# Merge exponents formed in the product's PSUM bank, and the masked statistics multiplied by GpSimd

## The chip, the core and the metric

The kernel runs on one core of one Trainium2 chip. The metric is the device time of one execution in microseconds; the figure of a kernel is the median of its runs. The engines are TensorE (PE, with its weight loads PEld), VectorE (DVE), ScalarE (ACT), GpSimd (POOL) and SyncE (SP), which here only issues transfers.

## The reference, cut to what matters

One decoder layer for a prompt of 2048 positions (width 1024) and a sample group of 8 x 4 positions: RMSNorm and one input projection, dilated attention with 8 heads of 64 and a spatial gating unit, an output projection, then a SwiGLU network and a final norm. In the attention each head has three branches, (window, dilation) = (128,1), (512,4), (2048,16), and merges them by their softmax denominators:

```python
def _merge_branches(outs, lses):
    w = jax.nn.softmax(jnp.stack(lses, axis=0), axis=0)
    return jnp.sum(w[..., None] * jnp.stack(outs, axis=0).astype(jnp.float32), axis=0)
```

The change touches how the weights of this merge are computed for the prompt.

## The kernel before, in words

The program has three parts in time: the projections with the sample group's attention and the gates (to about 600 us), the prompt's attention (about 600 to 975 us), and the output projection with the feed-forward network (to the end).

The prompt's attention runs head by head. Two kinds of items follow each other, one per step of a plan: a *band* item (the branches of dilation 1 and 4 together) for each of the 16 query tiles of a head, in which query rows are consecutive positions; and a *strided* item (dilation 16), four per head, each for four of the 16 residues, in which a row is a position divided by 16. For a band item TensorE forms the scores in one of two PSUM buffers ps_s (L864), VectorE adds the bias and takes the row's extremum (L870, an operation followed by a readout into the statistics st), ScalarE forms the exponential with its row sum (L875), TensorE transposes it (L891) into a PSUM bank, ScalarE and VectorE copy that out (L896, L902), and TensorE multiplies by the values (L916). For a strided item GpSimd first reorders k, qh and ql into sq (L937, three copies), TensorE forms the scores (L945), VectorE adds the bias (L950) and reduces (L952), GpSimd subtracts (L953), ScalarE takes the exponential (L956), VectorE sums (L960), TensorE transposes (L965) and multiplies (L974). A score buffer is free for the item after next when L870 (or L950) has read it.

The tile st of a head holds four statistics per row and tile: [0] and [1] for the band, by position tile, [2] and [3] for the strided branch, by residue. The class Stats brings both into one layout and computes the two merge factors of each position, in steps: **a** multiplies st[0:2], repeated eight times, by a mask sel_g into the tile sm (128 x 256, L998); **b** multiplies sm by sel_r on TensorE (L1004, four matmuls of 16 columns), which turns the band statistics into the strided layout, in one PSUM bank; **c** copies both to SBUF (s, L1008); **weights_a** forms the smaller of the two extrema and the two differences (L1014, L1015, L1016, tiles of 128 x 16); **weights_e** takes their exponentials on ScalarE (L1019); **weights_b** forms the weighted sum, its reciprocal and the two factors on VectorE (L1024 to L1028); **store** sends the factors to DRAM from ScalarE's queue (L1032). They are loaded back, spread over the partitions, by merge_load (L1042 or L1046), and merge applies them in three operations per quarter of a head (L1054, L1056, L1058), on GpSimd but for one quarter of the last head, whose result merge_store sends out on SyncE's queue (L1063).

The order is written by hand: `at(step, phase, function)` enters a call, and the calls are issued by step, then by phase (early, exp, low, scores, turn, mid, values, out, misc, store), then by entry. Each engine executes its share in that order. The statistics of a head are computed while the next head's items run; the last head's are computed in two halves, one of them during its own items. That makes nine calls.

A bank for transposes and for the product of step b comes from ps_a, which takes three banks in turn.

Of the kernel before, what the change touches and what calls it, by code (L numbers as in the profile page):

```python
# [13 lines left out]
OP = mybir.AluOpType  # L14
# [5 lines left out]
P = 128  # L20
T = 2048
NT = T // P
# [42 lines left out]
def hymba_step(ctx: ExitStack, tc: tile.TileContext, A: dict, O: dict):  # L65
    nc = tc.nc
    sync, act, dve, pool, pe = nc.sync, nc.scalar, nc.vector, nc.gpsimd, nc.tensor
# [7 lines left out]
    turn = [0, 0, 0, 0]  # L75
# [618 lines left out]
    for half in range(2):  # L694
        for ki, kind in enumerate(ORDER[half]):
            for gi, tiles in enumerate(GROUPS):
                start = ((half * 5 + ki) * 3 + gi) * 8
                for k in range(KD):
                    if start == 0:

                        for j in range(3):
                            n = 3 * k + j
# [281 lines left out]
    s12 = {}  # L984
# [3 lines left out]
    class Stats:  # L988
# [6 lines left out]
        def a(self):  # L995
            n = self.r1 // 8
            self.m = ap_.tile([P, 2 * P], F32, name="sm", tag="sm", bufs=1).rearrange("p (a n g) -> p a n g", a=2, g=8)[:, :, 0:n]
            dve.tensor_tensor(self.m, self.st["t"][:, 0:2, 0:n].unsqueeze(3).broadcast_to([P, 2, n, 8]),  # L998
                              sel_g.unsqueeze(1).unsqueeze(1).broadcast_to([P, 2, n, 8]), op=OP.mult)
# [6 lines left out]
        def c(self):  # L1006
            self.s = self.small("s12", 2)
            dve.tensor_copy(self.s.rearrange("p a t -> p (a t)"), self.p[0:self.r1, 0:2 * NT])  # L1008

        def weights_a(self):  # L1010

            m3 = self.st["t"][0:self.r1, 2, :]
            self.f = f = self.small("f", 3)
            dve.tensor_tensor(f[:, 2, :], self.s[:, 0, :], m3, op=OP.min)  # L1014
            dve.tensor_sub(f[:, 0, :], f[:, 2, :], self.s[:, 0, :])  # L1015
            dve.tensor_sub(f[:, 1, :], f[:, 2, :], m3)  # L1016
# [4 lines left out]
        def weights_b(self):  # L1021
            f, m = self.f, self.f[:, 2, :]
            dd = self.small("dd", 2)
            dve.tensor_mul(dd[:, 0, :], f[:, 0, :], self.s[:, 1, :])  # L1024
# [112 lines left out]
    def stats_of(h, steps, r0, r1):  # L1137
        d = {}
        at(*steps[0], lambda: d.update(s=Stats(h, sts[h], r0, r1)))
        for (y, ph), fn in zip(steps, "a b c weights_a weights_e weights_b store".split()):  # L1140
            at(y, ph, lambda fn=fn: getattr(d["s"], fn)())

    for h in range(H):
# [4 lines left out]
        if end:  # L1148

            x = s0 - NI  # L1150
            stats_of(h, [(x + y, ph) for y, ph in ((14, "early"), (14, "turn"), (15, "early"), (15, "misc"), (16, "early"), (16, "early"), (16, "mid"))], 0, 64)
            steps = ((2, "early"), (2, "turn"), (3, "early"), (4, "early"), (4, "early"), (5, "early"), (5, "early"))
# [6 lines left out]
        else:  # L1159
            steps = ((2, "misc"), (3, "misc"), (4, "early"), (4, "early"), (5, "early"), (5, "misc"), (6, "mid"))  # L1160
# [890 lines left out]
```

## Time and profile before

| | |
|---|---|
| median of 3 runs | 2692.8 us (2679.7 to 2697.14) |
| profiled execution, own time | 2691.25 us |
| its span, first to last instruction | 2689.5 us |
| mean granted TensorE clock | 0.967 |
| busy: PE, PEld, DVE, ACT, POOL | 2533.0, 2170.3, 1375.7, 1206.2, 1408.6 us |
| attention stage, 560 to 980 us: PE, DVE, POOL busy | 368.81, 259.14, 276.24 us |

The page is read in this way: busy time counts an instruction from its start to its end, so an instruction that stands at an engine and cannot proceed counts as busy too. Idle time ahead of a group is listed with the instruction that ended most of it. The granted clock is a share of full speed.

### The profile page before, as it was taken

The page shows a single profiled execution, that of the slowest core. Times are in us where ns is not written, and L with a number is a line of the kernel's source. Part 1 is how long each engine was busy: PE and PEld are TensorE (multiplying, and loading weights), DVE is VectorE, ACT ScalarE, POOL GpSimd, SP SyncE. Part 2 cuts the span into 40 slices and gives each one's busy share as a digit, 9 for nine tenths or more (in the row PEclk, how much of TensorE's full clock was granted, in tenths as well). Part 3 has the DMA queues.
Part 4 walks back from the last instruction along what each step waited for, and adds up shares of the span by engine and source line. Part 5 has one row for each costly group of instructions (what it writes and reads, how often), then busy time and mean ns, then how long its engine had stood idle before and what let it go on. Part 6 is the DMA issues. An engine that isn't in the chain of part 4 may idle for free. (4 is left out here: it accounts for less than half of the span.)

```text
span 2689.5 us, 38648 instructions
## 1 busy us (share of the span) xinstructions
PE 2533.0 (94%) x13578; PEld 2170.3 (81%) x13578; DVE 1375.7 (51%) x2724; ACT 1206.2 (45%) x2569; POOL 1408.6 (52%) x1048
## 2 busy tenths in 40 slices
PE   8998999999898877999999999999999998999997
PEld 6777777676665656999999987999999987999996
DVE  3268784436666664444444465444444455444445
ACT  6423344436666636545454545433232335433333
POOL 1036553224868753767676743545363533666663
PEclk9999999999999988899999999899999999899998
DMA  8765854675556374446364554436364543555653
GB/s 245 218 201 153 258 142 134 183 252 178 171 165 201 100 209 133 141 140 205 129 200 153 176 180 153 161 129 219 126 206 147 193 158 122 172 202 197 205 198 114
DMA packets 298165, 468.45 MB, mean 174 GB/s; under 512 B 26839, under 2 KB 163208, under 8 KB 292084
## 3 DMA queue, kind: packets, MB, share of 16 engines
q1 hardware_dynamic: 283588, 443.31, 51.4%
q10 hardware_dynamic: 14384, 22.68, 3.2%
q8 instruction: 108, 1.77, 0.3%
q14 instruction: 85, 0.70, 0.1%
HBM read 374.38 MB, written 161.64 MB: 199 GB/s over the span
## 5 line engine op out<-in xcount | busy, mean ns | idle before, releaser
L1496 POOL TENSOR_TENSOR op<-fr,op 128x512 fp32r<-128x512 f32 x385 | 489.1, 1300 | 318.5 <-ACT op L1492 297.2
L1553 PE MATMUL ps_m<-xh,op 128*128 128x384 f32 (+4 forms) x1932 | 629.6, 326 | 8.4 <-ACT xh L1430 5.3
L1554 PE MATMUL ps_m<-xl,op 128*128 128x384 f32 (+4 forms) x1932 | 627.8, 325 | 7.0 <-DVE xl L1433 7.0
L1555 PE MATMUL ps_m<-xh,op 128*128 128x384 f32 (+4 forms) x1932 | 627.5, 325 | 0.0
L1626 PE MATMUL ps_o<-dw,hw 128*128 128x512 f32 x2040 | 484.1, 392 | 9.3 <-DVE acc L1628 9.3
L1626 PEld LDWEIGHTS ps_o<-dw,hw 128*128 128x128 f32 x2040 | 379.7, 188 | 91.6 <-DVE acc L1628 16.0
L1553 PEld LDWEIGHTS ps_m<-xh,op 128*128 128x128 f32 x1932 | 377.4, 195 | 13.6 <-ACT xh L1430 5.9
L1554 PEld LDWEIGHTS ps_m<-xl,op 128*128 128x128 f32 x1932 | 377.9, 196 | 11.7 <-DVE xl L1433 7.7
L1555 PEld LDWEIGHTS ps_m<-xh,op 128*128 128x128 f32 x1932 | 377.1, 195 | 0.0
L1628 DVE TENSOR_TENSOR acc<-acc,ps_o 128x512 f32<-128x512 f32 (+1 forms) x362 | 247.0, 686 | 213.8 <-PE ps_o L1626 213.7
L1593 ACT ACTIVATE ps_t<-zn 128x384 f32<-128x384 f32 (+1 forms) x126 | 58.3, 463 | 480.5 <-DVE zn L1576 371.0
L1492 ACT ACTIVATE op<-fr 128x512 fp32r<-128x512 f32 x396 | 235.8, 622 | 21.1 <-DMA fr<-ab_d 17.7
L137 POOL TENSOR_TENSOR dw<-fd,dw 128x1024 fp32r<-128x1024 f32 x66 | 158.7, 2405 | 123.4 <-ACT dw L134 123.4
L317 PE MATMUL ps_s<-wh,xh 128*128 128x512 f32 x480 | 197.7, 412 | 6.4 <-ACT xh L134 6.1
L318 PE MATMUL ps_s<-wl,xh 128*128 128x512 f32 x480 | 191.9, 400 | 0.8 <-DVE wl L225 0.8
L319 PE MATMUL ps_s<-wh,xl 128*128 128x512 f32 x480 | 191.5, 399 | 0.0
L1496 POOL TENSOR_TENSOR op<-pair,op 128x512 fp32r<-128x512 f32 x63 | 81.4, 1298 | 117.3 <-ACT op L1492 117.3
L1603 ACT ACTIVATE hw<-ps_t 128x384 fp32r<-128x384 f32 (+1 forms) x126 | 56.1, 453 | 176.7 <-DVE ps_t L1599 175.8
L317 PEld LDWEIGHTS ps_s<-wh,xh 128*128 128x128 f32 x480 | 92.7, 193 | 36.2 <-issue 8.2
L603 POOL TENSOR_TENSOR vl<-kv,vh 100x512 fp32r<-100x512 f32 (+1 forms) x32 | 45.6, 1426 | 124.1 <-ACT vh L597 41.7
L319 PEld LDWEIGHTS ps_s<-wh,xl 128*128 128x128 f32 x480 | 92.5, 193 | 20.7 <-DVE xl L137 0.2
L318 PEld LDWEIGHTS ps_s<-wl,xh 128*128 128x128 f32 x480 | 93.1, 194 | 19.3 <-DVE wl L225 2.0
(451 smaller groups left out, 4575.5 us busy)
## 6 DMA issues: line engine op xcount, KB each, us to landing
fr<-ab_d SPq DMA_DIRECT2D x308, 256.0 KB
fd<-in_w_down_dram SPq DMA_DIRECT2D x66, 512.0 KB
out_ks_dram<-in_cache_k_dram SPq DMA_DIRECT2D x56, 512.0 KB
out_vs_dram<-in_cache_v_dram SPq DMA_DIRECT2D x56, 512.0 KB
ab_d<-fr SPq DMA_DIRECT2D x88, 256.0 KB
raw<-in_w_in_dram SPq DMA_DIRECT2D x72, 256.0 KB
qk_d<-pair SPq DMA_DIRECT2D x64, 256.0 KB
ab_d<-pair SPq DMA_DIRECT2D x63, 256.0 KB
```

The costliest lines, as they stand in the source:

```text
L137: (eng_lo or pool).tensor_sub(lo, src, hi.bitcast(F32))
L317: pe.matmul(o[j], xh[:, k, :], wh, start=(k == 0), stop=False)
L318: pe.matmul(o[j], xh[:, k, :], wl, start=False, stop=False)
L319: pe.matmul(o[j], xl[:, k, :], wh, start=False, stop=(k == KD - 1))
L1492: act.activation(ops[f, j][0], ab[f][j], AF.Copy)
L1496: (pool if f or j in POOL_LOW else dve).tensor_sub(lo_, ab[f][j], hi.bitcast(F32))
L1553: pe.matmul(out, wh[:, ks], xh[:, :, k], start=(k == 0), stop=False)
L1554: pe.matmul(out, wh[:, ks], xl[:, :, k], start=False, stop=False)
L1555: pe.matmul(out, wl[:, ks], xh[:, :, k], start=False, stop=(k == 3))
L1593: act.activation(g, c, AF.Silu)
L1626: pe.matmul(ps[0:nr], l_, r_[:, cs], start=(z == 0 and y == 0), stop=(z == FC - 1 and y == len(pairs) - 1))
L1628: dve.tensor_add(B.acc[i][0:nr, cs], B.acc[i][0:nr, cs], ps[0:nr])
```

## The change

The product of step a is issued on GpSimd instead of VectorE. Step c no longer copies the bank first: it subtracts the strided extremum from the band's in the product's own bank, into columns that the product leaves free (x), forms the two exponents from x (the smaller of -x and 0, the smaller of x and 0) in SBUF, and copies only the band's sums to SBUF. Step weights_a is gone; the four instructions of c stand where the copy stood. The lists of steps lose one entry. Behind L1016 the changed file has two lines less: L1022 to L1026 are the products that stand at L1024 to L1028 before, and GpSimd's L1052, L1054 and L1056 are the merge operations at L1054, L1056 and L1058 before.

```diff
         def a(self):
...
-            dve.tensor_tensor(self.m, self.st["t"][:, 0:2, 0:n].unsqueeze(3).broadcast_to([P, 2, n, 8]),
+            pool.tensor_tensor(self.m, self.st["t"][:, 0:2, 0:n].unsqueeze(3).broadcast_to([P, 2, n, 8]),
                               sel_g.unsqueeze(1).unsqueeze(1).broadcast_to([P, 2, n, 8]), op=OP.mult)
...
         def c(self):
-            self.s = self.small("s12", 2)
-            dve.tensor_copy(self.s.rearrange("p a t -> p (a t)"), self.p[0:self.r1, 0:2 * NT])
-
-        def weights_a(self):
-
-            m3 = self.st["t"][0:self.r1, 2, :]
+
+            p, m3, x = self.p[0:self.r1], self.st["t"][0:self.r1, 2, :], self.p[0:self.r1, 2 * NT:3 * NT]
+            self.s = self.small("s1", 1)[:, 0, :]
             self.f = f = self.small("f", 3)
-            dve.tensor_tensor(f[:, 2, :], self.s[:, 0, :], m3, op=OP.min)
-            dve.tensor_sub(f[:, 0, :], f[:, 2, :], self.s[:, 0, :])
-            dve.tensor_sub(f[:, 1, :], f[:, 2, :], m3)
+            dve.tensor_tensor(x, p[:, 0:NT], m3, op=OP.subtract)
+            dve.tensor_scalar(f[:, 0, :], x, -1.0, 0.0, op0=OP.mult, op1=OP.min)
+            dve.tensor_scalar(f[:, 1, :], x, 0.0, None, op0=OP.min)
+            dve.tensor_copy(self.s, p[:, NT:2 * NT])
...
-            dve.tensor_mul(dd[:, 0, :], f[:, 0, :], self.s[:, 1, :])
+            dve.tensor_mul(dd[:, 0, :], f[:, 0, :], self.s)
...
-        for (y, ph), fn in zip(steps, "a b c weights_a weights_e weights_b store".split()):
+        for (y, ph), fn in zip(steps, "a b c weights_e weights_b store".split()):
...
-            stats_of(h, [(x + y, ph) for y, ph in ((14, "early"), (14, "turn"), (15, "early"), (15, "misc"), (16, "early"), (16, "early"), (16, "mid"))], 0, 64)
-            steps = ((2, "early"), (2, "turn"), (3, "early"), (4, "early"), (4, "early"), (5, "early"), (5, "early"))
+            stats_of(h, [(x + y, ph) for y, ph in ((14, "early"), (14, "turn"), (15, "early"), (16, "early"), (16, "early"), (16, "mid"))], 0, 64)
+            steps = ((2, "early"), (2, "turn"), (3, "early"), (4, "early"), (5, "early"), (5, "early"))
...
-            steps = ((2, "misc"), (3, "misc"), (4, "early"), (4, "early"), (5, "early"), (5, "misc"), (6, "mid"))
+            steps = ((2, "misc"), (3, "misc"), (4, "early"), (5, "early"), (5, "misc"), (6, "mid"))
```

The order of instructions is the same as before on TensorE, ScalarE and SyncE. On VectorE, before, at the third head's call (e is the bias tile's output, pt the transposes' copy, ps_t_6814 the bank of the product, s_6819 its copy; an ISA pair is L870 and its readout):

```order
L870 ISA e,st<-ps_s,b 128x256
L870 ISA st 128x1
L998 TENSOR_TENSOR sm<-st,sel_g 128x256
L902 COPY pt<-ps_o_6786 128x2x128
L950 TENSOR_TENSOR e_6796<-ps_s,b 128x512
L952 TENSOR_REDUCE st<-e_6796 128x4
L1008 COPY s_6819<-ps_t_6814 128x32
L1014 TENSOR_TENSOR f<-s_6819,st 128x16
L1015 TENSOR_TENSOR f<-f,s_6819 128x16
L1016 TENSOR_TENSOR f<-f,st 128x16
L870 ISA e,st<-ps_s,b 128x384
```

And at the same place in the changed kernel:

```order
L870 ISA e,st<-ps_s,b 128x256
L870 ISA st 128x1
L902 COPY pt<-ps_o_6786 128x2x128
L950 TENSOR_TENSOR e_6796<-ps_s,b 128x512
L952 TENSOR_REDUCE st<-e_6796 128x4
L1011 TENSOR_TENSOR ps_t_6814<-ps_t_6814,st 128x16
L1012 TENSOR_SCALAR f<-ps_t_6814 128x16
L1013 TENSOR_SCALAR f<-ps_t_6814 128x16
L1014 COPY s_6819<-ps_t_6814 128x16
L870 ISA e,st<-ps_s,b 128x384
```

The product is gone from VectorE, and the four instructions between the row minimum and the next bias are others. On GpSimd, before, at the second head's call (o and ob are the merge's tiles, pair the loaded factors, e the strided item's exponents):

```order
L1054 TENSOR_TENSOR ob<-ob,pair 128x512
L1056 TENSOR_TENSOR o_5643<-o_5643,pair 64x32x16
L1058 TENSOR_TENSOR ob<-ob,o_5643 64x512
L953 TENSOR_TENSOR e_6322<-e_6322,st 128x512
L937 COPY sq<-k 128x512
```

And at the same place in the changed kernel:

```order
L1052 TENSOR_TENSOR ob<-ob,pair 128x512
L1054 TENSOR_TENSOR o_5643<-o_5643,pair 64x32x16
L998 TENSOR_TENSOR sm<-st,sel_g 128x256
L1056 TENSOR_TENSOR ob<-ob,o_5643 64x512
L953 TENSOR_TENSOR e_6322<-e_6322,st 128x512
L937 COPY sq<-k 128x512
```

The product stands between the second and the third operation of the last merge of the head before, whose lines bear other numbers. The third to sixth head are alike. At the first half of the last head's statistics GpSimd has, in the changed kernel (op are halves of the output projection's weights):

```order
L137 TENSOR_TENSOR op<-v,op 128x512
L1054 TENSOR_TENSOR o_8432<-o_8432,pair 64x32x16
L1056 TENSOR_TENSOR ob<-ob,o_8432 64x512
L998 TENSOR_TENSOR sm<-st,sel_g 128x2x64
L137 TENSOR_TENSOR op<-v,op 128x512
```

There the product stands behind a whole merge operation and ahead of a weight split.

## The prediction

> **What bounds the kernel now.** I read the engine shares on the page first, then the waits of the attention stage (560 to 980 us, where all nine calls of the statistics lie), then the instructions in order of time around one call.
>
> ```profile
> PE 2533.0 (94%) x13578; PEld 2170.3 (81%) x13578; DVE 1375.7 (51%) x2724; ACT 1206.2 (45%) x2569; POOL 1408.6 (52%) x1048
> ...
> L1496 POOL TENSOR_TENSOR op<-fr,op 128x512 fp32r<-128x512 f32 x385 | 489.1, 1300 | 318.5 <-ACT op L1492 297.2
> ```
>
> Those are the page's shares and its group of GpSimd's plain products (mean 1300 ns). The waits of the attention stage, total us, times and longest:
>
> ```profile
> PE ps_s L864 <- DVE st L870: 16.7, 13, 3.9
> ...
> PE ps_t L1004 <- DVE sm L998: 3.4, 1, 3.4
> ```
>
> TensorE is busy for 94% of the span, so only time in which it stands still can be won. In the attention stage it stands still for 16.7 us, 13 times, until VectorE frees a score bank with its bias instruction L870. VectorE is not full (51%); it is late at certain places. The statistics' own wait, L1004 for sm on a PSUM bank of the t kind, shows once, 3.4 us.
>
> ```profile
> L950 DVE TENSOR_TENSOR e<-ps_s,b 128x512 f32<-128x512 f32 x32 | 21.8, 680 | 1.7 <-PE ps_s L945 1.7
> L998 DVE TENSOR_TENSOR sm<-st,sel_g 128x256 f32<-128x256 f32 (+1 forms) x9 | 14.2, 1583 | 2.5 <-ACT e L875 2.5
> L1014 DVE TENSOR_TENSOR f<-s,st 128x16 f32<-128x16 f32 (+1 forms) x9 | 11.7, 1303 | 0.2
> ```
>
> These groups are VectorE's in the same stage (count, busy us, mean ns). L950 works on 512 columns with one input in PSUM and takes 680 ns; L1014 works on 16 columns with both inputs in SBUF and takes 1303 ns. So it is waiting while it counts as busy. The next rows, of the third head's call, show for what (start, duration, engine, line; in brackets the idle time ahead and who ended it).
>
> ```profile
> 732.13 1.61 POOL L1056 TENSOR_TENSOR o<-o,pair 64x512 f32<-64x512 f32 x1
> 733.82 1.51 POOL L1058 TENSOR_TENSOR ob<-ob,o 64x512 f32<-64x512 f32 x1
> 734.42 0.62 PE L1004 MATMUL ps_t<-sel_r,sm 128*128 128x16 f32 x4
> 735.08 0.19 DVE L1008 COPY s<-ps_t 128x32 f32<-128x32 f32 x1 [0.93 <-PE ps_t L1004]
> 735.29 1.04 POOL L953 TENSOR_TENSOR e<-e,st 128x512 f32<-128x512 f32 x1
> 735.30 1.09 DVE L1014 TENSOR_TENSOR f<-s,st 128x16 f32<-128x16 f32 x1
> 736.28 1.03 POOL L937 CAST sq<-k 128x512 fp32r<-128x512 f32 x1
> 736.43 0.94 DVE L1015 TENSOR_TENSOR f<-f,s 128x16 f32<-128x16 f32 x1
> 737.26 1.03 POOL L937 CAST sq<-qh 128x512 fp32r<-128x512 f32 x1
> 737.30 1.06 DVE L1016 TENSOR_TENSOR f<-f,st 128x16 f32<-128x16 f32 x1
> 738.23 1.06 POOL L937 CAST sq<-ql 128x512 fp32r<-128x512 f32 x1
> 738.28 0.55 DVE L870 CUSTOM_DVE_ANT_0 e<-ps_s,b 128x384 f32<-128x384 f32 x1
> 738.88 0.56 PE L864 MATMUL ps_s<-k,qh 128*128 128x384 f32 x2 [2.26 <-DVE st L870]
> 739.36 0.17 DVE L1024 TENSOR_TENSOR dd<-f,s 128x16 f32<-128x16 f32 x1
> 740.14 0.19 DVE L1028 TENSOR_TENSOR f<-f 128x32 f32<-128x32 f32 x1
> 740.85 0.81 DVE L870 CUSTOM_DVE_ANT_0 e<-ps_s,b 128x640 f32<-128x640 f32 x1
> ...
> 743.04 1.25 PE L945 MATMUL ps_s<-sq 128*128 128x128 f32 x8
> ```
>
> L1014, L1015 and L1016 each end within 0.1 us of the end of a GpSimd instruction (736.33, 737.31, 738.29) and do their short work between two of them. GpSimd never idles here, so the sequence from the copy to L1016 lasts from 735.08 to 738.28, 3.2 us, and TensorE waits 2.26 us at 738.88 for the L870 queued behind it. The later small products L1024 to L1028 have two SBUF inputs too, but start when GpSimd has just run dry (738.23 + 1.06 = 739.29): 0.97 us for all five.
>
> A stop of TensorE also costs clock. These are stretches of 3.41 us: bounds, length, TensorE's busy time, weight loads, VectorE, ScalarE, GpSimd, granted clock.
>
> ```profile
> 736.54:739.96 3.42, 1.16 (x9) 1.05 (x8) 3.35 (x10) 1.57 (x4) 2.75 (x3) 1.00 1.01 232
> 739.96:743.37 3.41, 3.41 (x20) 2.75 (x19) 2.51 (x7) 2.26 (x7) 0.00 (x0) 0.50 0.91 243
> 750.20:753.61 3.41, 2.00 (x19) 1.36 (x17) 1.76 (x4) 3.34 (x8) 0.82 (x1) 1.00 0.91 215
> 862.84:866.25 3.41, 2.00 (x18) 1.74 (x15) 2.09 (x3) 1.58 (x7) 3.41 (x4) 1.00 1.01 418
> 866.25:869.66 3.41, 3.41 (x12) 1.04 (x10) 1.71 (x3) 1.09 (x4) 3.33 (x3) 0.50 0.31 125
> ```
>
> After a stretch with 1.16 us of TensorE work the next one runs at 0.50; with 2.00 us it does so once (862.84) and once not (750.20). A stop of more than about 1.4 us in a stretch is therefore near the point where a half-clock stretch follows, worth up to 1.7 us (half of 3.41).
>
> **The change, part by part.**
>
> *The product sm on GpSimd.* Nine instructions leave VectorE, 14.2 us of its busy time. At the heads' calls VectorE waits for TensorE's transposes right after, so this gives nothing by itself. GpSimd gets nine. No row shows this form there. Bounds: 0.52 us (half of L953's 1.04 for 512 columns, also with a repeated operand) and 1.61 us (L1056 whole, the slowest form in the rows); I take 0.65, half of the 1300 ns that the plain L1496 takes for 512 columns, since it is the same operation with a plain output. In the third head GpSimd now reaches it when L1056 ends, at 733.74, or about 0.15 earlier since VectorE's product no longer cuts in ahead: ready at 734.25 to 734.4, and TensorE asks at 734.42. So no wait, cover under 0.2 us; at the 1.61 us bound L1004 starts some 0.9 us late in five heads. Behind it GpSimd's L1058, L953 and the three sq copies, and on SP the store of ob that waits for L1058, come 0.45 us later: the last sq ends at 739.75 instead of 739.29. TensorE uses it at 743.04, so that delay alone is covered.
>
> The Trainium skill, "GPSIMD Engine Reference", section Engine selection, speaks against this part: it puts elementwise work with two inputs on VectorE and calls GpSimd about two times slower. Applied to the 0.41 us that this product takes on VectorE when nothing is in its way, as in the first head, that is an estimate of 0.83 us, and by it the sum below would be about 1 us worse (0.2 us in each of five heads); no row here shows the form on GpSimd.
>
> *Exponents in PSUM.* A copy and three instructions with two SBUF inputs become four that each have at most one SBUF input. Nearest rows: the copy from PSUM, 0.19 us (L1008), L1024 at 0.17, and the step of the dependent chain L1024 to L1028, about 0.2 each. Together 0.75 us; bounds 0.5 us (overlapped) and 3.2 us (they wait as now). I take 0.75, because L950, one input in PSUM, holds its 680 ns on average, in the same stage beside the same GpSimd. VectorE is then at L870 at 735.08 + 0.75 = 735.85 instead of 738.28, done at 736.45, and TensorE, which ends its previous work at 736.6, hardly waits: 2.26 us freed in this head. The bank of the product is held for four instructions instead of one, to 735.85; the transposes that take it next start after 740, so that costs nothing.
>
> *Where the stall goes.* This is the step that decides. L870 runs twice (0.55 and 0.68 us with their readouts), so the small products, which were behind GpSimd's last copy, now start at 737.1, amid the copies, which run until 739.75. They are untouched and have two SBUF inputs. The seventh head shows today what happens then:
>
> ```profile
> 920.30 1.43 PE L945 MATMUL ps_s<-sq 128*128 128x128 f32 x8 [3.29 <-DVE e L950]
> ...
> 921.85 0.26 DVE L1024 TENSOR_TENSOR dd<-f,s 128x16 f32<-128x16 f32 x1
> 922.24 0.92 DVE L1026 TENSOR_TENSOR f<-dd 128x16 f32<-128x16 f32 x1
> 923.48 0.71 DVE L1028 TENSOR_TENSOR f<-f 128x32 f32<-128x32 f32 x1
> ```
>
> L1024 takes 0.26, the sum L1026 0.92 and the last product L1028 0.71 us: from 921.85 to 924.19, 2.34 us instead of 0.97. In the third head the three ends are those of the copies, 737.75, 738.75 and 739.75, so the products finish at 739.8 instead of 740.33. Behind them VectorE has a row sum (0.68) and the third L870 (0.81 and its readout), which frees the bank for the strided scores L945: 739.8 + 0.7 + 0.9 = 741.4. TensorE is there before 740.6, and waits. L945 moves from 743.04 to 741.4, by 1.65 us, and not by the whole 2.26 us with the half-clock stretch on top.
>
> *The other calls.*
>
> ```profile
> 650.44 1.04 POOL L937 CAST sq<-ql 128x512 fp32r<-128x512 f32 x1
> ...
> 654.97 1.08 PE L945 MATMUL ps_s<-sq 128*128 128x128 f32 x8 [0.70 <-DVE st L870]
> ...
> 784.93 0.56 PE L864 MATMUL ps_s<-k,qh 128*128 128x384 f32 x2 [1.61 <-DVE st L870]
> ...
> 787.87 1.08 PE L945 MATMUL ps_s<-sq 128*128 128x128 f32 x8
> ...
> 941.09 0.38 PE L1004 MATMUL ps_o<-sel_r,sm 128*64 128x16 f32 x4 [0.36 <-DVE sm L998]
> ...
> 942.48 1.55 POOL L1058 TENSOR_TENSOR ob<-ob,o 64x512 f32<-64x512 f32 x1
> ...
> 951.74 0.90 PE L864 MATMUL ps_s<-k,qh 128*128 128x384 f32 x2 [3.86 <-DVE st L870]
> ```
>
> First head: GpSimd is free ahead of sm, its copies still end at 651.48 (650.44 + 1.04) and only the first product meets them; L945 comes at about 654.0, 1.0 us earlier. Second, third and fifth head are alike, 1.65 to 1.9: 3 x 1.7 = 5.1 us. In the fourth and sixth TensorE ran a half-clock stretch before the call, reached it later, and lost only 1.61 us there (784.93); L945 (787.87) was about to be reached anyway, and moves by 0.9: 1.8 us. Seventh head: L945 at 920.30 waits 3.29 us, its cause falls away, but sm stands behind L953 in GpSimd's queue and delays L1004 by 0.4, and the products still contend: 2.2 us. Eighth head, first half: L1004 at 941.09 waited 0.36 us for VectorE; its product now stands behind L1058, which ends at 944.03, so TensorE stops for 3.4 us there, and in exchange the 3.86 us ahead of 951.74, for an L870 behind the same three instructions, go: 0.3 us won. Second half: the 3.4 us of L1004 stay and grow by 0.25, as GpSimd gets to sm only after a merge, and the merges behind sm on GpSimd come 0.5 later, through a store and a load that TensorE waits for near 977: 0.75 us lost.
>
> *New half-clock stretches.* The new stop of 1.3 to 1.6 us ahead of L945 is at the 1.4 us point. At one chance in three in the three heads that I credited with a full clock, at 1.5 us each: 1.6 us given back.
>
> Sum: -1.0 - 5.1 - 1.8 - 2.2 - 0.3 + 0.75 + 1.6 = -8.05 us. The stages behind have TensorE at 90% and more, and nothing there reads the clock time, so I carry the sum to the end. The profiled execution took 2691.25 us around a span of 2689.5; 2691.25 - 8 = 2683.2. It lies 1.55 below the median of the runs (2692.8), which reach from 2679.7 to 2697.1; between 2683.2 and 2692.8 - 8 = 2684.8 I forecast 2684.
>
> The Trainium skill, "TensorE: Matmul & The Clock Gate", section Part 1, has the clock halved after a whole idle window of about 3.4 us, so that gaps of 2.26 us would leave it alone. The rows differ: a window a third busy was followed by 0.50, and the measurement decides. By the page's rule the stretches at half clock would stay as they are, and three heads would win less: from 784.93 to 787.87 TensorE needs 2.94 us to L945 at full clock, so L945 would stand at 741.8 today, 0.45 us win each, a sum of about -6 with nothing given back.
>
> **The rivals.**
>
> *The stall goes for good.* If the small products slip through between GpSimd instructions, or GpSimd is done earlier, the heads keep the whole gap: 1.0 + 2.26 x 3 + 1.61 x 2 + 3.0 = 14 us, and 1.5 us for each of four half-clock stretches behind these gaps, 6: 2691 - 20 = 2671. For it speaks the size of the waits; against it the seventh head's rows and that the copies follow without a gap.
>
> *GpSimd becomes the late engine (slower).* If sm takes the 1.61 us bound there, L1004 starts 0.9 us late in five heads, the last copy ends 1 us later still and takes the small products with it, so the heads win nothing (739.8 becomes 740.8, later than the 740.33 of today), the seventh loses 1, and the eighth's L1004 stops a further 1 us in each half: 5 x 0.9 + 1 + 2 + 0.75 = 8 us, 2699. It decides from about 1.1 us, where L1026 to L1028 would end as late as now. For it: sm has two repeated operands and runs of eight elements, and L1056, with runs of sixteen, is the slow form. Against it: L953 has a repeated operand too, at 1.04 us for twice the columns.
>
> *Nothing changes.* If the instructions with a PSUM input wait as the old ones did (3.2 us), VectorE's chain stays and only sm moves: +0.75 + 1, 2693. L950's 680 ns speaks against it.
>
> **How the numbers follow.** Chances: my forecast 0.62 (own range 2678 to 2690), stall gone for good 0.18, GpSimd late 0.13, nothing changes 0.07. The range reaches to the first rival's side and over the third's: 2668 to 2696, which also takes in that single runs of this kernel lie 17 us apart. Faster by over 1% (27 us, about what a measurement of this kernel can tell from no change) needs more than every gap and half-clock stretch named here: 0.05. Slower by over 1% needs three times the slow rival: 0.02. Within 1%: 0.93.
>
> **What the changed profile would show.** Right: L1011 to L1014 in 0.7 to 0.9 us with no trace of GpSimd's beat; the L864 behind them waits under 0.5 us in heads two to six; L1022 to L1026 take 2 to 3 us in these heads; L945 waits 0.5 to 1.6 us for L870; sm about 0.65 us on GpSimd; one TensorE stop of about 3.4 us ahead of the eighth head's first L1004. Wrong: L1022 to L1026 in under 1.2 us (first rival), sm over 1.1 us and TensorE waiting for it in every head (second), or L1011 to L1013 near 1 us each (third). Half-clock stretches as many as before or more would take back what I credited.

## The result, and the profile after

| | before | changed |
|---|---|---|
| median of the runs | 2692.41 us (20 runs) | 2679.11 us (20 runs, 2670.92 to 2694.99) |
| ratio, 95% interval | | 0.9954 (0.9939 to 0.9969) |
| profiled execution, own time | 2691.25 us | 2674.03 us |
| its span | 2689.5 us | 2672.2 us |
| mean granted clock | 0.967 | 0.967 |

The kernel is faster by 12.4 us (8.3 to 16.4), by the ratio; the forecast was 8. One execution of the kernel before, 2825.57 us at a granted clock of 0.834, is kept out of every comparison below.

The attention stage first. The waits of the changed kernel, 560 to 980 us (us in total, times, longest):

```profile
PE ps_s L945 <- DVE st L870: 9.4, 6, 2.4
PE ps_t L1004 <- POOL sm L998: 5.7, 1, 5.7
PE ps_o L1004 <- POOL sm L998: 3.9, 2, 3.6
PE ps_s L864 <- DVE st L870: 2.8, 7, 1.5
```

The 16.7 us in which L864 waited for L870 are down to 2.8. In their place stand 9.4 us of L945 behind the third L870, and L1004, which waited 3.7 us for sm, now waits 9.6. The groups of the same stage (count, busy us, mean ns) show who holds VectorE now:

```profile
L1022 DVE TENSOR_TENSOR dd<-f,s 128x16 f32<-128x16 f32 (+1 forms) x9 | 16.1, 1792 | 3.1 <-ACT f L1017 3.1
L1023 DVE TENSOR_TENSOR dd<-f,st 128x16 f32<-128x16 f32 (+1 forms) x9 | 4.2, 467 | 0.0
...
L1011 DVE TENSOR_TENSOR ps_t<-ps_t,st 128x16 f32<-128x16 f32 x5 | 0.9, 182 | 8.1 <-PE ps_t L1004 8.1
...
L998 POOL TENSOR_TENSOR sm<-st,sel_g 128x256 f32<-128x256 f32 (+1 forms) x9 | 6.2, 687 | 4.9 <-ACT e L875 4.9
```

The four instructions of the exponents take 160 to 182 ns each in the mean, with no trace of the waits of L1014 to L1016 before. L1022, the first product with two SBUF inputs behind them, has the stall: 1792 ns in the mean. In the third head, in order of time:

```profile
734.05 0.18 DVE L1011 TENSOR_TENSOR ps_t<-ps_t,st 128x16 f32<-128x16 f32 x1 [2.18 <-PE ps_t L1004]
734.44 0.17 DVE L1014 COPY s<-ps_t 128x16 f32<-128x16 f32 x1
734.52 0.55 DVE L870 CUSTOM_DVE_ANT_0 e<-ps_s,b 128x384 f32<-128x384 f32 x1
734.86 1.05 POOL L937 CAST sq<-qh 128x512 fp32r<-128x512 f32 x1
735.61 1.36 DVE L1022 TENSOR_TENSOR dd<-f,s 128x16 f32<-128x16 f32 x1
735.86 1.07 POOL L937 CAST sq<-ql 128x512 fp32r<-128x512 f32 x1
...
738.29 0.81 DVE L870 CUSTOM_DVE_ANT_0 e<-ps_s,b 128x640 f32<-128x640 f32 x1
739.26 1.08 PE L945 MATMUL ps_s<-sq 128*128 128x128 f32 x8 [0.79 <-DVE st L870]
```

VectorE is at L870 0.47 us after L1011 begins. L1022 then starts inside the copies of sq, passes the end of the second (735.91) without doing its work, and ends at 736.97, when the last one ends (736.93). In the second, fourth and sixth head it lasts 2.0 us and L1023 another 1.1, and L945 waits 2.4 us. The last head:

```profile
940.63 1.51 POOL L1056 TENSOR_TENSOR ob<-ob,o 64x512 f32<-64x512 f32 x1
942.11 0.40 POOL L998 TENSOR_TENSOR sm<-st,sel_g 128x128 f32<-128x128 f32 x1
942.56 0.60 PE L1004 MATMUL ps_o<-sel_r,sm 128*64 128x16 f32 x4 [3.61 <-POOL sm L998]
...
965.36 1.39 POOL L1052 TENSOR_TENSOR ob<-ob,raw 128x512 f32<-128x512 f32 x1 [2.77 <-DMA raw<-f_d]
966.71 1.41 POOL L998 TENSOR_TENSOR sm<-st,sel_g 128x256 f32<-128x256 f32 x1
968.18 1.03 PE L1004 MATMUL ps_t<-sel_r,sm 128*128 128x16 f32 x4 [5.69 <-POOL sm L998]
```

In the first half sm stands behind the merge operation L1056, as forecast. In the second it stands behind L1052, which waits 2.77 us for the loaded factors: a transfer now holds up TensorE through GpSimd's queue. The product itself also takes 1.41 us there, where it takes 0.62 in the heads before.

That is the attention. TensorE runs the same 13,578 matmuls in the same order in every kernel of this study, so the start of each can be set against that of the same one in the profile of before. The feed-forward network works on three blocks of positions in turn; a *block change* is the stretch in which one block ends and the next begins. How much the difference grows in each stretch (us; by the time of before; minus is faster; "heads" are the first seven):

```
heads, 560 to 920                               -5.9
last head, 920 to 1030                          +4.6
feed-forward without its two block changes      -8.5
block changes, 1660 to 1740 and 2240 to 2340    -7.8
all other stretches                             +0.2
start of the last matmul                       -17.3
```

Of the 17.3 us, only 1.3 lie in the part of the program whose instructions the change touches. The feed-forward products, first before, then changed (shape, count, busy us and mean ns):

```profile
L1553 PE MATMUL ps_m<-xh,op 128*128 128x384 f32 x1176 | 399.0, 339 | 0.0
L1554 PE MATMUL ps_m<-xl,op 128*128 128x384 f32 x1176 | 398.7, 339 | 0.0
```

```profile
L1551 PE MATMUL ps_m<-xh,op 128*128 128x384 f32 x1176 | 395.4, 336 | 0.0
L1552 PE MATMUL ps_m<-xl,op 128*128 128x384 f32 x1176 | 394.9, 336 | 0.0
```

The same products, 3 ns shorter each. From 1150 us on, the starts of successive ones lie apart by (ns):

```
before   182 176 173 174 175 182 176 173 174 175 182 176 173 174 175
changed  173 173 174 173 173 174 173 173 174 172 174 173 174 173 174
```

Before, every fifth is late by some 9 ns; changed, none is. The block changes are another thing. The second of them (bounds, length, busy times of PE, PEld, DVE, ACT and POOL, granted clock), before and changed:

```profile
2240.00:2340.00 100.00, 92.61 (x533) 84.55 (x534) 45.07 (x131) 45.55 (x105) 44.47 (x34) 0.86 0.38 128
```

```profile
2240.00:2340.00 100.00, 93.82 (x629) 87.37 (x628) 48.28 (x139) 50.49 (x117) 56.21 (x42) 0.93 0.42 143
```

The changed kernel's execution had a clock of 0.93 there instead of 0.86, and the experiments below show that this clock differs between kernels with the same instructions too.

### The profile page after: what moved, and what is told of

The parts are those of the page before. It is cut to its first block, busy times and chain, and to the rows that moved or that the text cites. A ratio compares the mean times of both kernels' runs of the same rounds, so it can differ in the third digit from the quotient of the medians.

```text
span 2672.2 us, 38655 instructions
## 1 busy us (share of the span) xinstructions
PE 2518.1 (94%) x13578; PEld 2156.3 (81%) x13578; DVE 1355.1 (51%) x2715; ACT 1204.5 (45%) x2569; POOL 1411.5 (53%) x1057
## 5 line engine op out<-in xcount | busy, mean ns | idle before, releaser
L1551 PE MATMUL ps_m<-xh,op 128*128 128x384 f32 (+4 forms) x1932 | 621.8, 322 | 8.4 <-ACT xh L1428 5.4
L1552 PE MATMUL ps_m<-xl,op 128*128 128x384 f32 (+4 forms) x1932 | 620.3, 321 | 7.0 <-DVE xl L1431 7.0
L1553 PE MATMUL ps_m<-xh,op 128*128 128x384 f32 (+4 forms) x1932 | 620.6, 321 | 0.0
L1553 PEld LDWEIGHTS ps_m<-xh,op 128*128 128x128 f32 x1932 | 373.9, 194 | 0.0
L1626 DVE TENSOR_TENSOR acc<-acc,ps_o 128x512 f32<-128x512 f32 (+1 forms) x362 | 246.9, 686 | 213.4 <-PE ps_o L1624 213.4
```

The costliest lines, as they stand in the source:

```text
L1551: pe.matmul(out, wh[:, ks], xh[:, :, k], start=(k == 0), stop=False)
L1552: pe.matmul(out, wh[:, ks], xl[:, :, k], start=False, stop=False)
L1553: pe.matmul(out, wl[:, ks], xh[:, :, k], start=False, stop=(k == 3))
L1626: dve.tensor_add(B.acc[i][0:nr, cs], B.acc[i][0:nr, cs], ps[0:nr])
```

## The experiments

All times are medians; the ratio is to the kernel before on the same chip. "At equal clock" is the difference to before when the times of all 189 single runs are fitted with one level for each kernel and one slope on the run's mean granted clock (-1.9 us for +0.001, standard error 0.07); by it the changed kernel stands at -10.4 (within 1.3, as all these at 2 standard errors of 1.3 to 2.3). It takes out what the clock does by chance, but also what a kernel does to its own clock. The table of stretches, from one profile each, for all kernels but three that were run once:

```
                            heads  last head  feed-fwd  block ch.    end    raw ratio   at equal clock
changed                      -5.9     +4.6      -8.5      -7.8     -17.3     0.9954        -10.4
before, again                +3.1     +0.2      -0.4      +0.5      +4.9     0.9995         -1.8
sm on GpSimd only            +4.6     +4.3      -0.5      +0.7      +8.3     1.0041         +7.7
exponents only               -9.2     -1.8      -8.1      +0.4     -17.4     0.9924        -16.8
changed, padded              -4.8     +4.1      -0.6      +0.5      -1.4     0.9979         -1.5
before, op 128 B up          -1.0     +0.8      -7.8      +0.1      -5.6     0.9987         -7.3
before, op 128 B down        -1.0     +2.5      -7.7      +9.4      +0.7     0.9991         -8.4
changed, last head DVE       -4.7     -0.8      -7.3      -7.1     -21.2     0.9942        -14.7
exponentials in bank        -18.3     -6.9      -8.2      +3.4     -28.7     0.9899        -26.3
exponents only, bank turn    -9.2     +1.4      -8.0      +0.4     -11.6     0.9939        -16.3
```

Between the same two matmuls, a stretch can also be split into the time in which TensorE stands still and the time in which it is busy. The second grows when the clock is halved; "half clock" is the time at a granted clock of 0.50. "Before's order" are seven profiles: before, its repeat, and five versions of before that differ in addresses alone (us):

```
                           heads: still     busy      half clock   last head: still     busy
before's order           37.6 to 40.2  318.9 to 323.2  20.7 to 33.0   18.9 to 21.5  90.4 to 93.5
changed                      33.3         321.1           23.9            21.6          92.9
changed, padded              32.0         323.3           27.3            24.3          90.0
sm on GpSimd only            40.2         324.5           35.3            21.8          92.6
exponents only               29.4         321.6           24.2            19.3          88.9
exponents only, bank turn    29.4         321.6           24.2            16.5          94.8
changed, last head DVE       32.0         323.3           27.3            20.1          89.3
exponentials in bank         24.1         317.7           13.7            16.1          87.1
```

### The kernel before once more

> The kernel before, unchanged: a second profile of it. What is asked is how much of the gain between the two profiled executions (2689.5 us against 2672.2 us of span) lies in the feed-forward part, which the change does not touch, and whether that part differs by itself from one execution to the next. Theory A (the gain is made in the heads, by the stall that left L864; the feed-forward part varies by itself): the feed-forward products L1553 to L1555 come out of this second execution at 321 to 326 ns in the mean, somewhere between the two, and not where they were. Theory B (the smaller tile shifts the places of later tiles and the feed-forward products run faster for it): they come out at 325 to 326 ns again, and the feed-forward part takes as long as in the first profile of before within 2 us. Time: 2692 us, ratio 1.000, both theories.

2689.78 us, ratio 0.9995 (0.998 to 1.0011). The feed-forward products and their pattern of five are there again to the nanosecond (-0.4 us over the whole part). So that part does not vary by itself: theory A is wrong on this point. The heads do vary between two executions, by 3 us here, and most of that is busy time (323.2 us against 320.7), not standing still (40.2 against 39.6).

### The product on GpSimd alone

```diff
-            dve.tensor_tensor(self.m, self.st["t"][:, 0:2, 0:n]...
+            pool.tensor_tensor(self.m, self.st["t"][:, 0:2, 0:n]...
```

> Only the masked statistics' product on GpSimd; copy, minimum and two differences stay as they were. Theory A: the stall of L1014 to L1016 (1303, 1035 and 851 ns) and of L864 stays in the heads, and the last head still loses what it lost in the changed kernel (TensorE stops of 3.4 us or more ahead of L1004 in both halves, 3.61 and 5.69 us there), so it is slower than before by 3 to 7 us, ratio 1.001 to 1.003. Theory B, which has the tiles' size as the source of the gain: the size is that of before, so no gain, and the same loss in the last head, ratio 1.001 to 1.003 too. A rival to both (the product on GpSimd itself brings the gain, by freeing VectorE ahead of L864): faster, ratio 0.996 to 0.999.

2702.57 us, ratio 1.0041 (1.0025 to 1.0056): slower by some 11 us, more than either theory gave (7.7 at equal clock). Its waits in 560 to 980 us:

```profile
PE ps_s L864 <- DVE st L870: 17.4, 13, 3.6
PE ps_t L1004 <- POOL sm L998: 6.4, 1, 6.4
PE ps_o L1004 <- POOL sm L998: 3.6, 1, 3.6
```

The two stops of the last head are there (+4.3 us in that stretch). The seven heads are 4.6 us longer as well, but this one profile does not show that GpSimd's product did it: TensorE stands still there for 40.2 us, as in executions of before's order, and what lies outside their range is its busy time and its 35.3 us at half clock. The stall of L864 is no shorter without VectorE's product, so the rival, that freeing VectorE brings the gain, is out.

### The exponents alone

The change without its first diff line; the product stays on VectorE.

> Only the exponents made in the PSUM bank, the masked statistics' product stays on VectorE. Theory A: the release in the heads of 5 to 6 us stays and the loss of 5 to 7 us in the last head goes, so this is faster than the changed kernel by 4 to 7 us: 2673 to 2675 us, ratio to before 0.993 to 0.994. Theory B: the same in the heads and the feed-forward part as fast as in the changed kernel, so the same time, with the feed-forward products at 321 to 322 ns where A lets them lie anywhere in 321 to 326. Rival (the product on GpSimd is a part of the release in the heads, and without it the last head is no better): 2679 to 2682 us, ratio 0.995 to 0.996.

2670.37 us, ratio 0.9924 (0.9898 to 0.995): faster than the changed kernel, as theory A said, with the feed-forward products as fast as there, as B said. The intervals of the two ratios just overlap; at equal clock the kernels lie 6.4 us apart, beyond their errors. In the heads TensorE stands still for 29.4 us instead of 37.6 to 40.2, with the busy time unchanged, so the 9.2 us won there are stops that went. Its groups and waits in 560 to 980 us:

```profile
L1022 DVE TENSOR_TENSOR dd<-f,s 128x16 f32<-128x16 f32 (+1 forms) x9 | 11.7, 1305 | 2.2 <-ACT f L1017 2.2
```

```profile
PE ps_s L945 <- DVE st L870: 4.6, 5, 1.9
PE ps_t L1004 <- DVE sm L998: 4.4, 1, 4.4
```

With sm off GpSimd the copies of sq are through earlier, L1022 waits 1305 ns instead of 1792, and L945 4.6 us instead of 9.4.

### The changed kernel with the old allocation

```diff
-            self.s = self.small("s1", 1)[:, 0, :]
+            self.s = self.small("s1", 2)[:, 0, :]
```

> The changed kernel with the tile of the second sums allocated as large as the tile it replaced (2 x 16 numbers instead of 16, of which the second half is unused), so that all later tiles lie where they lay in the kernel before. Theory B: the feed-forward products are back at 325 to 326 ns, and most of the gain is gone: 2688 to 2692 us, ratio to before 0.998 to 1.000. Theory A: the places do not matter, 2679 us, ratio 0.995 to 0.996, as the changed kernel.

2685.53 us, ratio 0.9979 (0.9964 to 0.9994), and only 1.5 us under before at equal clock. The instructions are those of the changed kernel; only addresses differ. The pattern of five is back (339 to 340 ns), the feed-forward gain is gone (-0.6 instead of -8.5), and heads and last head do what they did. B's range was 0.998 to 1.000: at its edge.

### The place of the weights, in the kernel before

In the built programs the tiles op, the split feed-forward weights that L1553 to L1555 load into TensorE, begin at byte 149,856 of a partition before and at 149,984 in the changed kernel, because s1 takes 128 bytes less than s12 did. Nothing else that these products read has moved. Five versions of before move op, and with it the tiles that lie behind it, and change no instruction: 128 bytes up, 128 down, 64 down, 256 down and 64 up, in this order.

```diff
-            self.s = self.small("s12", 2)
+            self.s = hsmall("s12", 2 * NT, 1)[0:self.r1].rearrange("p (a t) -> p a t", a=2)
+            self.s = self.small("s12", 3)[:, 0:2, :]
+            self.s = hsmall("s12", 40, 2)[0:self.r1, 0:2 * NT].rearrange(...)
+            self.s = self.small("s12", 4)[:, 0:2, :]
+            self.s = hsmall("s12", 48, 1)[0:self.r1, 0:2 * NT].rearrange(...)
```

> The kernel before with one edit: the tile s12 has one buffer instead of two. It frees 128 bytes of each partition, and all tiles that are laid down behind it, the feed-forward weights op among them, lie where they lie in the changed kernel (byte 149,984 of a partition instead of 149,856). No instruction is added, removed or moved. Theory B (the place of op sets the speed of the feed-forward products): L1553 to L1555 at 336 and 289 ns instead of 339 and 291, starting 173 ns apart each instead of in a pattern of 173, 174, 175, 182, 176, and 6 to 8 us off the time: 2684 to 2686 us, ratio 0.997 to 0.998. Theory A (the place plays no part; the gain came from the order of the statistics): as before, 2692 us, ratio 1.000.

> The kernel before with the tile s12 taken one third larger than it uses, so that op lies 128 bytes to the other side, at byte 149,728. No instruction differs. If what counts is whether the place is an odd or an even multiple of 128 bytes away, the products are as fast as in the changed kernel: 2684 to 2686 us, ratio 0.997 to 0.998. If each shift towards lower places makes them slower, or if the places play no part, 2692 us or above, ratio 1.000 or more.

> The kernel before with the tile s12 taken larger, so that op lies 64 bytes lower, at byte 149,792. No instruction differs. What is read is the mean of L1553 to L1555 with 384 columns: 339 ns at byte 149,856 and 335 to 336 at 128 bytes above and below. If a period of 128 or 256 bytes with few slow places is behind it, 336 here; if the slow places fill half of the period, 339 or a value between.

> The kernel before with the tile s12 taken twice as large as it needs, so that op lies 256 bytes lower, at byte 149,600. No instruction differs. If the pattern has a period of 256 bytes, the products L1553 to L1555 with 384 columns take 339 ns as at byte 149,856; if byte 149,856 is a single bad place, or the period is longer, 336 ns.

> The kernel before with the tile s12 smaller and in one buffer, so that op lies 64 bytes higher, at byte 149,920. No instruction differs. With a period of 256 bytes and 339 ns at 149,856 against 336 at 149,984, a value between, 336.5 to 337.5 ns as at 149,792, if the speed goes by the distance to the slow place; 339 or 336 if it steps.

The products of 384 columns on L1553 in these five, in the same sequence:

```profile
L1553 PE MATMUL ps_m<-xh,op 128*128 128x384 f32 x1176 | 395.4, 336 | 0.0
```

```profile
L1553 PE MATMUL ps_m<-xh,op 128*128 128x384 f32 x1176 | 394.8, 336 | 0.0
```

```profile
L1553 PE MATMUL ps_m<-xh,op 128*128 128x384 f32 x1176 | 396.1, 337 | 0.0
```

```profile
L1553 PE MATMUL ps_m<-xh,op 128*128 128x384 f32 x1176 | 399.5, 340 | 0.0
```

```profile
L1553 PE MATMUL ps_m<-xh,op 128*128 128x384 f32 x1176 | 396.0, 337 | 0.0
```

Slow at 149,856 and 256 bytes below it, fast 128 bytes to either side, between at 64 bytes to either side: a dependence on the place with a period of 256 bytes, as far as six places tell. In the feed-forward part the five gain 7.8, 7.7, 4.4, 1.1 and 7.0 us. Theory B holds for the products. For the whole time it is less plain: the versions with op 128 bytes up and down were timed at 2687.2 and 2691.52 us, ratios 0.9987 (0.9964 to 1.001) and 0.9991 (0.9968 to 1.0014), less than the 6 to 8 us expected, and their intervals include both 1 and 0.997. Half of their runs had a clock of 0.957 to 0.962, as few runs of before had (mean 0.9642 and 0.9629 against 0.9657). Where that comes from shows at the block changes. The version 128 bytes down and the one 256 bytes down:

```profile
2240.00:2340.00 100.00, 94.67 (x500) 87.86 (x499) 40.51 (x120) 40.81 (x94) 41.77 (x32) 0.76 0.33 108
```

```profile
2240.00:2340.00 100.00, 93.88 (x475) 86.66 (x475) 38.79 (x121) 44.46 (x101) 43.48 (x33) 0.73 0.37 125
```

0.73 to 0.93 in the same 100 us, with slow products and with fast ones: over the profiles the block changes come out at about 0, -7 or +10 us. At equal clock the two versions are 7.3 and 8.4 us faster than before, the amount in their products. Whether shorter products make a low clock there more frequent, or chance gave these two kernels more such runs, stays open. The versions 64 and 256 bytes away were run once each, and only their products are used.

### The last head's product on VectorE

```diff
-            pool.tensor_tensor(self.m, self.st["t"][:, 0:2, 0:n]...
+            (dve if self.h == H - 1 else pool).tensor_tensor(self.m, self.st["t"][:, 0:2, 0:n]...
```

> The changed kernel with the masked statistics' product of the last head's two halves back on VectorE, the other seven on GpSimd. Theory (the product on GpSimd costs only in the last head, where it stands behind the merges): the stops ahead of L1004 of 3.61 and 5.69 us fall to 0.4 and about 3.4, and the time falls to that of the kernel with all nine on VectorE, 2669 to 2673 us, ratio 0.992 to 0.993. Rival (it costs in the other heads too, since the merges and the copies behind it on GpSimd come 0.45 us later): half of the loss stays, 2674 to 2677 us, ratio 0.9935 to 0.9945.

2673.07 us, ratio 0.9942 (0.9919 to 0.9964). The last head's two L1004:

```profile
938.50 0.38 PE L1004 MATMUL ps_o<-sel_r,sm 128*64 128x16 f32 x4 [0.36 <-DVE sm L998]
...
963.38 1.01 PE L1004 MATMUL ps_t<-sel_r,sm 128*128 128x16 f32 x4 [3.93 <-DVE sm L998]
```

The stops are 0.36 and 3.93 us instead of 3.61 and 5.69, and the last head's +4.6 us become -0.8. The heads stay at -4.7, not at the -9.2 of the exponents alone. Between the theory and the rival: the last head holds the larger, plainer part of the loss, the other heads some 4 us in the profiles. Of these, 2.6 us are time in which TensorE stands still (32.0 against 29.4), and the rest is busy time, which varies by itself. The two ratios' intervals overlap, and at equal clock the kernels differ by 2.1 us, which is within the errors.

### The exponentials in a bank too

On top of the exponents alone (product on VectorE):

```diff
         def weights_e(self):
-            act.activation(self.f[:, 0:2, :], self.f[:, 0:2, :], AF.Exp)
+            self.q = ps_a()[0:self.r1, 0:3 * NT].rearrange("p (a t) -> p a t", a=3)
+            act.activation(self.q[:, 0:2, :], self.f[:, 0:2, :], AF.Exp)
...
-            dve.tensor_mul(dd[:, 0, :], f[:, 0, :], self.s)
-            dve.tensor_mul(dd[:, 1, :], f[:, 1, :], self.st["t"][0:self.r1, 3, :])
-            dve.tensor_add(m, dd[:, 0, :], dd[:, 1, :])
+            dve.tensor_mul(dd[:, 0, :], q[:, 0, :], self.s)
+            dve.tensor_mul(q[:, 2, :], q[:, 1, :], self.st["t"][0:self.r1, 3, :])
+            dve.tensor_add(m, dd[:, 0, :], q[:, 2, :])
...
-            dve.tensor_mul(f[:, 0:2, :], f[:, 0:2, :], m...
+            dve.tensor_mul(f[:, 0:2, :], q[:, 0:2, :], m...
```

> The exponents made in the product's bank, all masked products on VectorE, and in addition the exponentials written to a PSUM bank, so that none of the small products L1022 to L1026 has both inputs in SBUF. It computes the same. Theory (the rest of the stall is in these products because GpSimd is busy beside their two SBUF inputs): each of them takes 0.2 us at every call, the waits of L945 for L870 fall from 4.6 us in sum to under 2, and the time lies 3 to 6 us under that of the kernel with the exponents alone, 2664 to 2668 us, ratio 0.990 to 0.991. Rival (TensorE is taken up by the next wait anyway, for the sq copies of GpSimd, 15.6 us in that kernel, or for the bank held by the exponentials): the products are short, but the time is the same, 2669 to 2672 us, ratio 0.992 to 0.993.

2661.03 us, ratio 0.9899 (0.9878 to 0.9919): the fastest of all, 15 us under the changed kernel by the ratios and 16 at equal clock. Its products (one line further down) and its waits for L870:

```profile
L1023 DVE TENSOR_TENSOR dd<-ps_t,s 128x16 f32<-128x16 f32 x6 | 1.0, 170 | 0.0
L1024 DVE TENSOR_TENSOR ps_t<-ps_t,st 128x16 f32<-128x16 f32 x6 | 1.1, 183 | 0.2
L1025 DVE TENSOR_TENSOR f<-dd,ps_t 128x16 f32<-128x16 f32 x6 | 1.0, 171 | 0.2
```

```profile
PE ps_s L864 <- DVE st L870: 1.3, 6, 0.4
...
PE ps_s L945 <- DVE st L870: 0.4, 1, 0.4
```

With one input in PSUM the same products take 170 to 183 ns, and the heads win 18.3 us: twice what the exponents gave, and more than the 3 to 6 us expected, which counted only the 4.6 us of waits for L870. Against the exponents alone TensorE stands still 5.3 us less in the heads, which is about those waits. Its busy time there is 3.9 us shorter, with 13.7 us at half clock instead of 24.2; whether the shorter stops brought that, as the prediction's reading of the clock would have it, rests on this one profile. The rival, that the next wait takes it all, is out: at equal clock the kernel lies 9.5 us under the exponents alone.

### Only the turn of the banks

The version with the exponentials in a bank also moves the turn of the three banks on by one. This one is the exponents alone, with that step added.

```diff
         def weights_e(self):
+            turn[2] = (turn[2] + 1) % 3
```

> The kernel with the exponents alone (all masked products on VectorE), in which the turn of the three banks is moved on by one where the exponentials are taken, as it is moved on by the bank that the exponentials get in the fastest kernel so far; nothing is written there. Theory (that kernel won by short products, not by another turn of the banks): the products L1022 to L1026 still wait for GpSimd, the stretch from 560 to 920 us stays 9 us under that of the kernel before, and the time is that of the exponents alone, 2669 to 2673 us, ratio 0.992 to 0.993. Rival (the turn of the banks, which decides which bank a transpose waits for, made a part of it): 2662 to 2667 us, ratio 0.989 to 0.991.

2673.01 us, ratio 0.9939 (0.9915 to 0.9962), heads -9.2 us, L1022's counterpart at 1311 ns: as the exponents alone. The turn of the banks is not what made the gain.

## Why the prediction was right in its number, and where it was not

The forecast was 2684 us and the result 2679.11, in the range. But it got there by two errors of opposite sign, and that is luck. At the addresses of before the same edit is worth 5.7 us (1.6 to 9.7) by the ratio, and 1.5 at equal clock and 1.4 in its profile.

- *Exponents in PSUM, 0.75 us:* the mechanism was right, the size a little large: L870 follows 0.47 us after L1011 in the third head, at the lower bound and under the 0.7 to 0.9 us that were to show it. L864's waits for L870 went from 16.7 to 2.8 us.
- *Where the stall goes:* right, and it was the step that decided. L1022 to L1026 took the stall over, 2.2 us in the third and fifth head as forecast, but about 3.7 us in the second, fourth and sixth. L945 waits for the third L870: 0.70 us in the first head, then 2.4 and 0.8 us in turn, where the text had 1.3 to 1.6. The exponentials in a bank show the cause, because there only the second SBUF input goes, and the version with the turn of the banks takes away its rival.
- *The first seven heads, -10.1 us, and +1.6 for new half-clock stretches* (one chance in three, three heads and 1.5 us make 1.5): for the exponents alone this was the right size (-9.2 in two profiles; the five versions of before with moved weights and the repeat spread from -2.9 to +3.1 around -0.7). The changed kernel has -5.9 and, padded, -4.8. Stretches at half clock fill 24 us of the heads in both kernels of the pair, 27 in the padded one, and 21 to 33 in executions of before's order, so whether the forecast 1.6 us came back cannot be told.
- *The product sm on GpSimd, priced at nothing in the heads:* the first step that failed. Its length was right (620 ns in the seven heads of the version with the last head on VectorE, forecast 0.65 us), and TensorE waits for it there in the seventh alone, 0.34 us for the forecast 0.4. But "that delay alone is covered" was wrong: the copies of sq end later, the small products that wait for them too, and L945 behind these. On top of the exponents it costs 3.3 to 4.5 us in the heads, of which 2.6 to 3.9 are time in which TensorE stands still (32.0 to 33.3 against 29.4). Without the exponents in PSUM no such loss is shown.
- *The eighth head, -0.3 and +0.75:* the second place of the same step. The first stop came as forecast (3.61 for 3.4 us). Of the 3.86 us that were to go in exchange, 1.5 stayed, because L1022 and L1024 wait there too. The second stop is 5.69 instead of 3.65 us: I had put 0.25 us on a merge operation ahead of sm, and did not ask how long that operation itself waits. It is 2.77 us, for a load, and 3.95 in the padded kernel. The last head's stretch came out at +4.6 (padded +4.1) for the 0.45 forecast. More time at half clock is not the reason: the changed kernel has 34 us of it there and before has 24, but the padded one loses as much with 24, in 24.3 us of standing still instead of 18.9 to 21.5. Alone, sm makes the kernel some 11 us slower, 7.7 at equal clock. My rival of a late GpSimd had that size, 8 us, but tied it to sm being long in every head (1.1 us or more); it was 0.62 us there, and 1.41 once, in the last call of the changed kernel.
- *"I carry the sum to the end":* the second step that failed. The tile of the sums takes 128 bytes less (64 in each of two buffers), the feed-forward weights moved, and their products became 3 ns shorter: -8.5 us in the changed kernel's profile. I had looked for changed instructions in that part and found none; I did not look at addresses.

Terms together, from the profiles: exponents about -10 (heads -9.2 and last head -0.2 in the mean of two, against -0.7 and +1.4 in the six of before's order), sm about +8 to +9 (4 in the heads, 4.6 in the last), the place about -8. That is -9 to -10, against -12.4 (8.3 to 16.4) measured and -10.4 at equal clock. The changed kernel's own profile shows -17.3 because its block change near 2290 us ran at a clock of 0.93.

The half of the edit that loses is the product on GpSimd; the exponents alone beat the whole by 6.4 us at equal clock, and with the exponentials in a bank as well the kernel runs 2661.03 us.

## What to carry to other kernels

When an instruction is moved to a queue off the critical path, look at what the instruction ahead of it in that queue waits for, and at everything behind it that others wait for. When a small VectorE chain crawls beside a busy GpSimd, give every one of its instructions an input in PSUM, not only the first ones: half a repair moves the stall to the next pair of SBUF inputs. And before a gain or a loss is put down to an edit, pad the buffers so that all addresses stay where they were: here 128 bytes of small tiles were worth some 8 us, and the edit at unchanged addresses 1.5 at equal clock.

## What the runs showed of the hardware that was not expected

- The pace of a stream of weight loads and matmuls depends on where the weights lie: 173 ns per product, or a pattern of five with one of 182, with a period of 256 bytes in the weights' place (336 ns against 339 to 340 in the mean, 64 bytes off 337). The products of 512 columns on L1626, which load their weights from another tile, stay at 391 to 392 ns in all of these. The Trainium skill, "TensorE: Matmul & The Clock Gate", section Step-by-step: what each phase is for, says that loading the next weights does not take read bandwidth from the running matmul; these runs show that their place still counts. What lies behind it was not found.
- A VectorE instruction with two SBUF inputs does not always get its turn at the next end of a GpSimd instruction. In the seventh head L1022 stood for 4.84 us, until 919.55, across four instructions of GpSimd that followed on the one running when it came:

```profile
914.46 1.07 POOL L937 CAST sq<-ql 128x512 fp32r<-128x512 f32 x1
914.71 4.84 DVE L1022 TENSOR_TENSOR dd<-f,s 128x16 f32<-128x16 f32 x1
915.46 1.07 POOL L953 TENSOR_TENSOR e<-e,st 128x512 f32<-128x512 f32 x1
916.44 1.07 POOL L937 CAST sq<-k 128x512 fp32r<-128x512 f32 x1
917.42 1.11 POOL L937 CAST sq<-qh 128x512 fp32r<-128x512 f32 x1
918.44 1.07 POOL L937 CAST sq<-ql 128x512 fp32r<-128x512 f32 x1
```

- The prediction had every one of them end at the next copy's end. The Trainium skill, "SBUF — State Buffer", section Who interferes with whom, has the pair contend, with the one that comes first blocking the other, and an instruction with at most one SBUF input, outside the two-port modes, go free. 170 ns against 1305 to 1792 agrees with the second. The 4.84 us show that the one that waits can lose several times in a row, also to instructions that start after it came.
- The same 100 us around a block change ran at a clock of 0.73 to 0.93 from one profile to the next, among kernels with the same instructions at 0.73 to 0.86; only one kernel was profiled twice, and there the difference was small (0.5 us). Over the profiles this and the other block change differ by 18 us in sum; the runs of one kernel lie 11 to 29 us apart.
